# Keys and values held for four query heads, and a position bias kept only where it varies, in a two-layer hybrid attention trunk

## The chip, the cores and the metric

The kernel runs on one core of a Trainium2 chip. The metric is the device time of one execution in microseconds (us); lower is better. The kernel is written against a scheduler that gets instructions in program order, decides in which order each engine runs them, and adds every wait.

## What is computed

The reference is a trunk of two layers over a sequence of 2048 tokens of width 1024, all in float32. Layer 0 mixes tokens in two ways side by side, and only these two matter here. `A` is sliding-window attention with 8 query heads and 2 key/value heads, so four query heads share one pair of keys and values. `B` has 8 heads with keys and values of their own; each 64-token chunk attends to itself and to 8 chunks before it, and a learned bias is added that depends only on the clipped distance.

```python
A_Q_HEADS, A_KV_HEADS, A_WINDOW = 8, 2, 128
B_HEADS, B_PREV_CHUNKS, B_MAX_REL = 8, 8, 128
...
# A: the keys and values of head h // 4, plus a learned sink per head
scores = einsum('bcqhgd,bclhd->bchgql', qc, kb) / sqrt(64)
probs  = softmax(concat([scores, sink]))[..., :-1]
...
# B: bias by distance, clipped to -128 .. 128
rel    = clip(qpos[:, None] - kpos[None, :], -128, 128) + 128
scores = einsum('bcqhd,bclhd->bhcql', qc, kb) / sqrt(64) + rel_table[:, rel]
probs  = softmax(where(valid, scores, -1e30))
```

Layer 1 is differential attention over the whole prefix; the change does not touch it.

## The kernel before

**Stages.** `project(0)` writes queries, keys, values and gates of layer 0 to DRAM scratch tensors. `_mix0` (line 505) then does the attention of layer 0 and its output projection. `project(1)` and `_mix1` do layer 1. Every float32 operand of a matmul is split into a high part H and a low part L, and products are summed over the parts.

**Blocks, heads, rounds.** `_mix0` goes through four blocks of 512 tokens (`b` 0 to 3; `NTB` is 4 tiles of 128). In each it visits 16 heads in rounds of four: two of A, two of B (`heads()`, line 768). Below, A6 and A7 are the A heads of a block's last round and B6, B7 its B heads; B5 is the head just before A6.

**One head.** `load_q` (line 524) loads the queries twice over: `mqd` holds the high parts in both halves of the partitions, `mql` the low parts in both, with two DMAs each. `load_k` (line 536) loads the high parts of the keys into one half of `mks` and the low parts into the other; which half is the high one goes with the parity of the head. `score` (line 544) makes one piece of scores with two matmuls, first with `mqd` (line 547), then with `mql` (line 548). `scores_a` (line 577) loads `mks` and the values `mvA` for every A head. `scores_b` (line 655) loads `mks`, `mvB` and a 128x640 bias, lets POOL write the two masked corners into the bias (lines 667 and 668), and for each 128-token row adds the bias and takes the row's maximum in one DVE instruction per piece (line 682, into `mSP`). ACT then takes the exponential into `mPB` (line 691), POOL scales it (line 693). `values_a` and `values_b` transpose the probabilities on PE (`mtrA` line 640, `mtrB` line 708), split the transposed tile into `mptH` on ACT and `mptL` on DVE (lines 553, 554), and multiply with the values (`mOA`, `mOB`).

**Buffers.** All loads are issued by SP's one queue, in order. A tile with the same tag waits for the release of the tile that many allocations earlier: `qd` has 3 buffers, `ql` 2, `ks` 2, `v` 2 (A and B share `ks` and `v`), `bias` 2, `SP` 2, `PB` 7, `ptH` and `ptL` 4 each. So the `mql` of a head waits for the scores of the head two before it.

**Order.** `pace` (line 48) interleaves three streams: the scores of the heads, the values trailing them by `LAG0` = 9 units, and side work: the last gate products of `project(0)` (`mlg`) and the output projection (`mom`) of finished blocks. The scheduler may still reorder.

Of the kernel before, what the change touches and what calls it, by code (L numbers as in the profile page):

```python
# [10 lines left out]
F32 = mybir.dt.float32  # L11
F32R = mybir.dt.float32r
AF = mybir.ActivationFunctionType
ALU = mybir.AluOpType
# [4 lines left out]
P = 128  # L19
# [4 lines left out]
BLK = NTB * P  # L24
NB = S // BLK
HD = 64
EPS = 1e-6
NEG = -1e30
# [3 lines left out]
def f32(ap):  # L32
    return ap.bitcast(F32)
# [52 lines left out]
class Trunk:  # L86
# [418 lines left out]
    def _mix0(self, es):  # L505
        nc, tc, a, s = self.nc, self.tc, self.a, self.s0
# [26 lines left out]
            nc.sync.dma_start(f32(ql[HD:P, :]), s[L][h // 2, r, tok])  # L533
            res["q"] = (qd, ql)

        def load_k(H, L, p, row, e, k0, k1):

            r = slice(row * HD, (row + 1) * HD)
            ks = ld.tile([P, 1024], F32R, tag="ks", name=n + "ks")
            nc.sync.dma_start(f32(ks[e * HD:(e + 1) * HD, :k1 - k0]), s[H][p, r, k0:k1])  # L540
            nc.sync.dma_start(f32(ks[(1 - e) * HD:(2 - e) * HD, :k1 - k0]), s[L][p, r, k0:k1])
            return ks

        def score(ps, q, j, ks, c0, c1):
            qd, ql = q
# [2 lines left out]
            self.anchor = nc.tensor.matmul(ps, ql[:, js], ks[:, c0:c1], start=False, stop=True).ins  # L548

        def split_pt(ps, wd, tag):  # L550
            H = sb.tile([P, 512], F32R, tag="ptH", name=n + "ptH", bufs=4)
            L = sb.tile([P, 512], F32R, tag="ptL", name=n + "ptL", bufs=4)
            nc.scalar.activation(H[:, :wd], ps[:, :wd], AF.Copy)
            nc.vector.tensor_tensor(L[:, :wd], ps[:, :wd], f32(H[:, :wd]), ALU.subtract)
            return H, L
# [19 lines left out]
            return yH, yL  # L575

        def scores_a(h, b, res):
            g, e = h // 4, h % 2
            k0, k1 = max(0, b * BLK - P), (b + 1) * BLK
# [3 lines left out]
            nc.sync.dma_start(  # L583
                f32(vt[:, :(k1 - k0) // P, :]),
                s["av"][k0:k1, g * 192:(g + 1) * 192].rearrange("(t p) c -> p t c", p=P),
            )
            nm, l, es_, r = small("anm", 4), small("al", 4), small("aes", 4), small("ar", 4)
            pt = sb.tile([P, NTB, 256], F32, tag="PA", name=n + "PA")
            for z in range(2):
# [63 lines left out]
                ys[h // 2] = finish(yt, (h // 2) * P, b)  # L653

        def scores_b(h, b, res):
            e = h % 2
            k0, k1 = max(0, (b - 1) * BLK), (b + 1) * BLK
            load_q("bqH", "bqL", h, b, res)
            ks = load_k("bkH", "bkL", h // 2, e, e, k0, k1)
# [7 lines left out]
            nc.gpsimd.memset(bias[0:HD, 576:640], NEG)  # L667
            nc.gpsimd.memset(bias[HD:P, 0:64], NEG)
            probs = res["p"] = []
            res.update(v=vt, k0=k0)  # L670
            for j in range(NTB):
                t = b * NTB + j
                w0 = max(0, 4 - t) * P
                wd = 640 - w0
                kc = (t - 4) * P + w0 - k0
                sp = sb.tile([P, 640], F32, tag="SP", name=n + "SP")
                cuts = [(0, 320), (320, 640)] if w0 == 0 else [(w0, 640)]
                m, nm, l, r = small("bm", 2), small("bnm"), small("bl"), small("br")
                for z, (ca, cz) in enumerate(cuts):
                    ps = pS.tile([P, 512], F32, tag="S", name=n + "SB")[:, :cz - ca]  # L680
                    score(ps, res["q"], j, ks, kc + ca - w0, kc + cz - w0)
                    nc.vector.tensor_tensor_reduce(
                        sp[:, ca:cz], ps, bias[:, ca:cz], 1.0, NEG, ALU.add, ALU.max, m[:, z:z + 1]
                    )
# [6 lines left out]
                nc.scalar.activation(pb[:, w0:640], sp[:, w0:640], AF.Exp, bias=nm, accum_out=l)  # L691
# [446 lines left out]
def _layout(inputs):  # L1138
# [11 lines left out]
    a["relb"] = np.ascontiguousarray(a.pop("ev_b_rel_bias")[:, rel])  # L1150
    return {k: np.ascontiguousarray(v) for k, v in a.items()}


# [14 lines left out]
```

## Time and profile before

| what | value |
|---|---|
| median of 3 runs | 2955.78 us (2952.22 to 2972.79) |
| the profiled execution, its own time | 2951.96 us |
| its span | 2950.2 us |
| mean granted TensorE clock | 0.972 |
| busy: PE, DVE, ACT, POOL | 2718.6, 1917.2, 1593.5, 1604.6 us |
| DMA traffic | 580.79 MB, mean 197 GB/s |
| heads of `_mix0`, first score to last score | 604.5 to 1152.9 us |
| first scores of the blocks | 604.5, 713.5, 859.4, 1005.5 us |

Times within the trace count from the start of the span. A row of the windows view has, for one stretch, each engine's busy time and number of instructions, the granted TensorE clock as a share of full speed, the share of time in which the DMA engines were busy, and what they moved. A row of the waits view says which group of instructions waited for which other group, for how long in all, how often, and how long at most. In the timeline, the bracket behind a row is the idle time of its engine before it and what ended it. Tile names carry the stage (`m` is `_mix0`); `mks<-akL` is the load of the low parts of A's keys into `mks`.

### The profile page before, as it was taken

The numbers are of one execution on the slowest core, as the hardware profiler recorded it, in microseconds if no ns is written. First come the engines' busy times: TensorE is split into PE (matmuls) and PEld (weight loads), VectorE is DVE, ScalarE is ACT, GpSimd is POOL, SyncE is SP. The second block draws the span as 40 slices with busy tenths as digits, with TensorE's granted clock in tenths as the row PEclk, the third lists the DMA queues.
The fourth block names the chain that finished last, engine by engine and source line by source line (L and its number), as shares of the span: only waits on it lengthen the run. The fifth ranks groups of instructions, "written<-read, shape, count | busy, mean of one in ns | idle before, by whom it ended". The sixth has DMA issues, their size and how long they took to land.

```text
span 2950.2 us, 45159 instructions
## 1 busy us (share of the span) xinstructions
PE 2718.6 (92%) x13672; PEld 2242.1 (76%) x13672; DVE 1917.2 (65%) x4652; ACT 1593.5 (54%) x4135; POOL 1604.6 (54%) x1966
## 2 busy tenths in 40 slices
PE   6999999988888889899999998889999999899888
PEld 5888888876777788777788886667777777677667
DVE  7752385266677676498818861665766888878752
ACT  4443543367556565243334331666766777778752
POOL 3541251245345343267745650776777878789851
PEclk9999999999999999999999998999999999999999
DMA  4773343669988886475895455576768777668863
GB/s 149 230 250 120 113 147 120 197 192 249 262 214 212 216 217 170 146 270 197 259 302 191 127 162 158 164 217 197 225 193 234 200 225 214 176 169 243 221 215 114
DMA packets 427537, 580.79 MB, mean 197 GB/s; under 512 B 48160, under 2 KB 198688, under 8 KB 427296
## 3 DMA queue, kind: packets, MB, share of 16 engines
q1 hardware_dynamic: 427296, 577.92, 66.7%
q8 instruction: 109, 1.79, 0.3%
q14 instruction: 132, 1.08, 0.1%
HBM read 413.14 MB, written 164.63 MB: 196 GB/s over the span
## 4 chain that ended last, share of the span: by engine, by line
PE 63%; DMA 15%; DVE 11%; ACT 4%; POOL 3%; issue 3%; SPq 2%; DVEq 0%; ACTq 0%; POOLq 0%
PE p1mm L216 4%; PE p1mm L214 4%; PE p1mm L215 4%; PE p0mm L215 3%; PE p0mm L216 3%; PE p0mm L214 3%; PE cS L865 3%; PE ctr L912 3%; PE cS L866 3%; DMA mks<-bkL 2%; PE cO L920 2%; PE cG L214 2%; PE cG L216 2%; PE com L214 2%; DVE cnm L869 2%
## 5 line engine op out<-in xcount | busy, mean ns | idle before, releaser
L872 ACT ACTIVATE cP<-cS,cnm 128x512 f32<-128x512 f32 (+3 forms) x640 | 399.0, 630 | 173.8 <-DVE cnm L869 96.0
L869 DVE TENSOR_REDUCE cnm<-cS 128x1 f32<-128x512 f32 (+3 forms) x640 | 374.3, 600 | 100.6 <-PE cS L866 95.4
L865 PE MATMUL cS<-ck,cqd 128*128 128x512 f32 (+3 forms) x640 | 262.9, 415 | 60.0 <-ACT cP L872 20.5
L304 POOL TENSOR_TENSOR p0wL<-p0ws,p0wH 128x512 fp32r<-128x512 f32 (+1 forms) x128 | 155.3, 1246 | 276.0 <-ACT p0wH L303 266.4
L216 PE MATMUL p1mm<-p1wH,p1hL 128*128 128x512 f32 x768 | 303.3, 395 | 0.0
L215 PE MATMUL p1mm<-p1wL,p1hH 128*128 128x512 f32 x768 | 302.9, 395 | 0.4 <-POOL p1wL L304 0.4
L214 PE MATMUL p1mm<-p1wH,p1hH 128*128 128x512 f32 x768 | 302.3, 395 | 0.8 <-ACT p1wH L303 0.8
L899 POOL TENSOR_TENSOR cP<-cP,cP 128x512 f32<-128x512 f32 (+3 forms) x256 | 285.2, 1135 | 0.3
L304 POOL TENSOR_TENSOR p1wL<-p1ws,p1wH 128x512 fp32r<-128x512 f32 x128 | 168.0, 1333 | 136.8 <-ACT p1wH L303 97.5
L214 PE MATMUL p0mm<-p0wH,p0hH 128*128 128x512 f32 (+1 forms) x640 | 237.6, 374 | 3.5 <-ACT p0vt L454 2.6
L866 PE MATMUL cS<-ck,cql 128*128 128x512 f32 (+3 forms) x640 | 235.3, 372 | 3.3 <-DMA cql<-qL 3.3
L215 PE MATMUL p0mm<-p0wL,p0hH 128*128 128x512 f32 (+1 forms) x640 | 238.2, 373 | 0.0
L216 PE MATMUL p0mm<-p0wH,p0hL 128*128 128x512 f32 (+1 forms) x640 | 237.7, 372 | 0.1
L916 DVE TENSOR_TENSOR cptL<-ctr,cptH 128x512 fp32r<-128x512 f32 (+1 forms) x320 | 190.7, 599 | 62.4 <-ACT cptH L915 61.4
L865 PEld LDWEIGHTS cS<-ck,cqd 128*128 128x128 f32 x640 | 123.2, 193 | 104.4 <-ACT cP L872 51.2
L915 ACT ACTIVATE cptH<-ctr 128x512 fp32r<-128x512 f32 (+1 forms) x320 | 169.6, 539 | 58.2 <-PE ctr L912 57.0
L893 POOL TENSOR_SCALAR cP<-cP,ccs 128x512 f32<-128x512 f32 (+3 forms) x288 | 191.9, 683 | 0.0
L912 PE MATMUL ctr<-ident,cP 128*128 128x128 f32 x1088 | 175.4, 277 | 1.4 <-POOL cP L899 1.2
L898 POOL TENSOR_SCALAR cP<-cP,ccs 128x512 f32<-128x512 f32 (+3 forms) x256 | 174.0, 693 | 0.0
L214 PEld LDWEIGHTS p1mm<-p1wH,p1hH 128*128 128x128 f32 x768 | 145.3, 189 | 29.9 <-ACT p1wH L303 1.2
L215 PEld LDWEIGHTS p1mm<-p1wL,p1hH 128*128 128x128 f32 x768 | 145.2, 189 | 29.9 <-POOL p1wL L304 0.8
L216 PEld LDWEIGHTS p1mm<-p1wH,p1hL 128*128 128x128 f32 x768 | 145.4, 189 | 29.3 <-issue 0.2
(321 smaller groups left out, 7719.0 us busy)
## 6 DMA issues: line engine op xcount, KB each, us to landing
p1ws<-in_od_w_in_dram SPq DMA_DIRECT2D x56, 512.0 KB, 4.7
p0ws<-in_ev_w_in_dram SPq DMA_DIRECT2D x48, 512.0 KB, 4.3
ck<-kH SPq DMA_DIRECT2D x160, 128.0 KB, 4.0
ck<-kL SPq DMA_DIRECT2D x160, 128.0 KB, 4.2
cvH<-vH SPq DMA_DIRECT2D x80, 256.0 KB, 3.9
cvL<-vL SPq DMA_DIRECT2D x80, 256.0 KB, 4.7
cqd<-qH SPq DMA_DIRECT2D x128, 128.0 KB, 4.9
cql<-qL SPq DMA_DIRECT2D x128, 128.0 KB, 4.7
```

The lines of the kernel that those rows point to most:

```text
L214: mm(ps, aH, bH, start=first, stop=False)
L215: mm(ps, aH, bL, start=False, stop=False)
L216: mm(ps, aL, bH, start=False, stop=last)
L304: nc.gpsimd.tensor_tensor(l[:, :width], ws[:, k, :width], f32(h[:, :width]), ALU.subtract)
L865: mm(ps, qd[:, m, js], kt[:, :wd], start=True, stop=False)
L866: self.anchor = mm(ps, ql[:, m, js], kt[:, :wd], start=False, stop=True).ins
L869: nc.vector.tensor_reduce(nm[:, m, z:z + 1], ps, AX.X, ALU.max, negate=True)
L872: nc.scalar.activation(chunks[z][:, :wd], ps, AF.Exp, bias=nm[:, m, z:z + 1], accum_out=acc)
L893: nc.gpsimd.tensor_scalar(p1, p1, c1, 1.0, ALU.mult, ALU.mult)
L899: nc.gpsimd.tensor_tensor(p1, p1, p2, ALU.add)
L912: nc.tensor.transpose(tp[:, (j - j0) * P:(j - j0 + 1) * P], us[j][kt // 4][:, kk:kk + P], self.ident)
L916: nc.vector.tensor_tensor(L[:, :wd], tp[:, :wd], f32(H[:, :wd]), ALU.subtract)
```

## The change

Two things change in `_mix0`, and one in the host's table.

1. **A's keys and values.** `load_group` loads them into tiles of their own, `mksA` and `mvA`, with one buffer each, when the first of the four heads that share them comes; the other three use the same tiles. The high parts now always lie in the lower half. `mks` and `v` are left to B.
2. **B's bias.** For distances over 128 the clipped bias is one number per head. The kernel subtracts that number from the whole row (a softmax does not see it), so the first 384 of 640 columns need no bias but the mask, which is one shared tile `edge`. Only 256 columns are loaded per head; POOL subtracts the head's number (`far`, loaded once and negated once by DVE) from them and masks one corner. The row of scores is cut at column 384 (384 and 256 wide) instead of 320, and in block 0, where a row is shorter, two of the four rows now come in two pieces where they came in one. The DVE writes its sum straight into `PB`, the exponential works in place, and the `SP` tile is gone.
3. **Buffers.** `PB` goes from 7 to 8, `ptH` and `ptL` from 4 to 3 each.

```diff
+        edge = ld.tile([P, 384], F32, tag="edge", name=n + "edge", bufs=1)
+        far = ld.tile([P, 8], F32, tag="far", name=n + "far", bufs=1)
+        nc.gpsimd.memset(edge, 0.0)
+        nc.gpsimd.memset(edge[HD:P, 0:64], NEG)
+        nc.sync.dma_start(far, a["relfar"].to_broadcast([P, 8]))
+        nc.vector.tensor_scalar(far, far, -1.0, None, ALU.mult)
+        group = {}
+
+        def load_group(b, g):
+            k0, k1 = max(0, b * BLK - P), (b + 1) * BLK
+            ks = ld.tile([P, 640], F32R, tag="ksA", name=n + "ksA", bufs=1)
+            load_k(ks, "akH", "akL", 0, g, k0, k1)
+            vt = ld.tile([P, 5, 192], F32R, tag="vA", name=n + "vA", bufs=1)
+            nc.sync.dma_start(
+                f32(vt[:, :(k1 - k0) // P, :]),
+                s["av"][k0:k1, g * 192:(g + 1) * 192].rearrange("(t p) c -> p t c", p=P),
+            )
+            return ks, vt, k0
...
-            H = sb.tile([P, 512], F32R, tag="ptH", name=n + "ptH", bufs=4)
-            L = sb.tile([P, 512], F32R, tag="ptL", name=n + "ptL", bufs=4)
+            H = sb.tile([P, 512], F32R, tag="ptH", name=n + "ptH", bufs=3)
+            L = sb.tile([P, 512], F32R, tag="ptL", name=n + "ptL", bufs=3)
...
             load_q("aqH", "aqL", h, b, res)
-            ks = load_k("akH", "akL", 0, g, e, k0, k1)
-            vt = ld.tile([P, 5, 192], F32R, tag="v", name=n + "vA")
...
+            if h % 4 == 0:
+                group[g] = load_group(b, g)
+            ks, vt, k0 = group[g]
...
-            bias = ld.tile([P, 640], F32, tag="bias", name=n + "bias")
+            bias = ld.tile([P, 256], F32, tag="bias", name=n + "bias")
             nc.sync.dma_start(bias, a["relb"][h])
-            nc.gpsimd.memset(bias[0:HD, 576:640], NEG)
-            nc.gpsimd.memset(bias[HD:P, 0:64], NEG)
+            nc.gpsimd.tensor_scalar(bias, bias, 1.0, far[:, h:h + 1], ALU.mult, ALU.add)
+            nc.gpsimd.memset(bias[0:HD, 192:256], NEG)
...
-                sp = sb.tile([P, 640], F32, tag="SP", name=n + "SP")
-                cuts = [(0, 320), (320, 640)] if w0 == 0 else [(w0, 640)]
+                pb = sb.tile([P, 640], F32, tag="PB", name=n + "PB", bufs=8)
+                cuts = [(w0, 384), (384, 640)] if w0 < 384 else [(w0, 640)]
...
-                    nc.vector.tensor_tensor_reduce(
-                        sp[:, ca:cz], ps, bias[:, ca:cz], 1.0, NEG, ALU.add, ALU.max, m[:, z:z + 1]
-                    )
+                    by = edge[:, ca:cz] if ca < 384 else bias[:, ca - 384:cz - 384]
+                    nc.vector.tensor_tensor_reduce(pb[:, ca:cz], ps, by, 1.0, NEG, ALU.add, ALU.max, m[:, z:z + 1])
...
-                pb = sb.tile([P, 640], F32, tag="PB", name=n + "PB", bufs=7)
-                nc.scalar.activation(pb[:, w0:640], sp[:, w0:640], AF.Exp, bias=nm, accum_out=l)
+                nc.scalar.activation(pb[:, w0:640], pb[:, w0:640], AF.Exp, bias=nm, accum_out=l)
```

**What moves on SP's queue.** The place is the last round of block 2, from the moment the scores of B5 are done: the loads for A7 and B6. Before (`mqd_11935` and `mql_11938` are the queries of B6, `mql_11859` those of A7, `mks_11862` and `mks_11941` the keys of A7 and B6):

```order
L529 DMA mqd_11935<-bqH_62 64x512
L532 DMA mql_11859<-aqL_58 64x512
L533 DMA mql_11859<-aqL_58 64x512
L540 DMA mks_11862<-akH_59 64x640
L487 DMA x1_84<-mxr_11506 128x512
L583 DMA mvA_11304<-av_61 128x5x192
L541 DMA mks_11862<-akL_60 64x640
L530 DMA mqd_11935<-bqH_62 64x512
L532 DMA mql_11938<-bqL_63 64x512
L533 DMA mql_11938<-bqL_63 64x512
L540 DMA mks_11941<-bkH_64 64x1024
L661 DMA mvB_11383<-bv_66 128x8x128
```

Now (`mqd_11827` and `mql_11830` are the queries of B6, `mql_11756` those of A7, `mks_11833` the keys of B6):

```order
L539 DMA mks_11833<-bkH_64 64x1024
L676 DMA mvB_11293<-bv_66 128x8x128
L540 DMA mks_11833<-bkL_65 64x1024
L681 DMA mbias_11838<-in_relb_dram 128x256
L529 DMA mqd_11827<-bqH_62 64x512
L532 DMA mql_11756<-aqL_58 64x512
L533 DMA mql_11756<-aqL_58 64x512
L676 DMA mvB_11492<-bv_66 128x8x128
L487 DMA x1_84<-mxr_11414 128x512
L530 DMA mqd_11827<-bqH_62 64x512
L532 DMA mql_11830<-bqL_63 64x512
L533 DMA mql_11830<-bqL_63 64x512
```

A7 has no loads of keys and values left, and B6's keys stand ahead of A7's queries instead of behind B6's.

**What moves on PE.** The place is where A7 begins in the same round. Before, the last rows up to A7's first score (ahead of these, behind B5's last score, stand 12 rows of `mom`, 8 score matmuls of A6, 5 of `mOB` and 15 `mtrA`):

```order
L647 MATMUL mOA<-mptH,mvA 128x128
L649 MATMUL mOA<-mptL,mvA 128x128
L647 MATMUL mOA<-mptH,mvA 128x256
L649 MATMUL mOA<-mptL,mvA 128x256
L647 MATMUL mOA<-mptH,mvA 128x256
L649 MATMUL mOA<-mptL,mvA 128x256
L647 MATMUL mOA<-mptH,mvA 128x256
L649 MATMUL mOA<-mptL,mvA 128x256
L647 MATMUL mOA<-mptH,mvA 128x128
L649 MATMUL mOA<-mptL,mvA 128x128
L640 MATMUL mtrA<-ident,mPA 128x128
L547 MATMUL mSA<-mks,mqd 128x256
```

Now (ahead of these, behind B5's last score, stand 3 rows of `mom`, 8 score matmuls of A6, 2 of `mOB` and 4 `mtrA`):

```order
L567 MATMUL mSA<-mksA,mqd 128x256
L656 MATMUL mtrA<-ident,mPA 128x128 x4
L214 MATMUL mom<-mw,myH 128x512
L215 MATMUL mom<-mw,myH 128x512
L216 MATMUL mom<-mw,myL 128x512
L214 MATMUL mom<-mw,myH 128x512
L215 MATMUL mom<-mw,myH 128x512
L216 MATMUL mom<-mw,myL 128x512
L214 MATMUL mom<-mw,myH 128x512
L215 MATMUL mom<-mw,myH 128x512
L216 MATMUL mom<-mw,myL 128x512
L568 MATMUL mSA<-mksA,mql 128x256
```

A7's scores stand earlier: the ten `mOA` matmuls that stood between B5 and A7 now come behind A7's first scores, so there is less PE work between the end of B5's scores and the first matmul that needs A7's `mql`.

**What moves on DVE.** The place is the first row of B6. Before, the sum goes to `mSP` and stands between the splits of the transposed tiles:

```order
L554 TENSOR_TENSOR mptL_11651<-mtrB_11645,mptH_11650 128x512
L682 ISA mSP_11950,mbm_11951<-mSB_11955,mbias_11946 128x320
L682 ISA mbm_11951 128x1
L554 TENSOR_TENSOR mptL_11666<-mtrB_11660,mptH_11665 128x512
L682 ISA mSP_11950,mbm_11951<-mSB_11959,mbias_11946 128x320
L682 ISA mbm_11951 128x1
```

Now it goes to `mPB_11842`, the buffer that the first row of B4 held until its last transpose (`mtrB_11634` below is that transpose's output):

```order
L574 TENSOR_TENSOR mptL_11570<-mtrB_11564,mptH_11569 128x512
L582 TENSOR_TENSOR myt_11112<-mOA_11451,mlow_11543 64x512
L574 TENSOR_TENSOR mptL_11597<-mtrB_11592,mptH_11596 128x384
L698 ISA mPB_11842,mbm_11843<-mSB_11847,medge_6097 128x384
L698 ISA mbm_11843 128x1
L698 ISA mPB_11842,mbm_11843<-mSB_11851,mbias_11838 128x256
L698 ISA mbm_11843 128x1
L574 TENSOR_TENSOR mptL_11612<-mtrB_11608,mptH_11611 128x256
L574 TENSOR_TENSOR mptL_11637<-mtrB_11634,mptH_11636 128x128
```

The sum of B6's first row has moved behind three splits of B4's values, and two more splits stand behind it.

More of the change, by code (lines that the diff above doesn't have):

```diff
@@ L534, in load_q, with load_k @@
             res["q"] = (qd, ql)
-        def load_k(H, L, p, row, e, k0, k1):
+        def load_k(ks, H, L, p, row, k0, k1):
             r = slice(row * HD, (row + 1) * HD)
-            ks = ld.tile([P, 1024], F32R, tag="ks", name=n + "ks")
-            nc.sync.dma_start(f32(ks[e * HD:(e + 1) * HD, :k1 - k0]), s[H][p, r, k0:k1])
-            nc.sync.dma_start(f32(ks[(1 - e) * HD:(2 - e) * HD, :k1 - k0]), s[L][p, r, k0:k1])
-            return ks
+            nc.sync.dma_start(f32(ks[0:HD, :k1 - k0]), s[H][p, r, k0:k1])
+            nc.sync.dma_start(f32(ks[HD:P, :k1 - k0]), s[L][p, r, k0:k1])
+            return ks
+        edge = ld.tile([P, 384], F32, tag="edge", name=n + "edge", bufs=1)
[15 more added lines that the diff above has]
+            return ks, vt, k0
         def score(ps, q, j, ks, c0, c1):
@@ L577, in scores_a @@
         def scores_a(h, b, res):
-            g, e = h // 4, h % 2
-            k0, k1 = max(0, b * BLK - P), (b + 1) * BLK
+            g = h // 4
             load_q("aqH", "aqL", h, b, res)
-            ks = load_k("akH", "akL", 0, g, e, k0, k1)
-            vt = ld.tile([P, 5, 192], F32R, tag="v", name=n + "vA")
-            nc.sync.dma_start(
-                f32(vt[:, :(k1 - k0) // P, :]),
-                s["av"][k0:k1, g * 192:(g + 1) * 192].rearrange("(t p) c -> p t c", p=P),
-            )
+            if h % 4 == 0:
+                group[g] = load_group(b, g)
+            ks, vt, k0 = group[g]
             nm, l, es_, r = small("anm", 4), small("al", 4), small("aes", 4), small("ar", 4)
@@ L655, in scores_b @@
         def scores_b(h, b, res):
-            e = h % 2
             k0, k1 = max(0, (b - 1) * BLK), (b + 1) * BLK
             load_q("bqH", "bqL", h, b, res)
-            ks = load_k("bkH", "bkL", h // 2, e, e, k0, k1)
+            ks = load_k(ld.tile([P, 1024], F32R, tag="ks", name=n + "ks"), "bkH", "bkL", h // 2, h % 2, k0, k1)
             vt = ld.tile([P, 8, P], F32R, tag="v", name=n + "vB")
```

4 lines of the change are left out of this document (2 added, 2 removed).

## The prediction

> **What bounds the kernel now.** Only `_mix0` changes, so I first read the stage view for where it lies and how busy each engine is in it (block 0, blocks 1 to 3, the tail of the output projection, then `project(1)` beside them).
>
> ```profile
> core 0: us, PE busy (x) PEld busy (x) DVE busy (x) ACT busy (x) POOL busy (x), PEclk, DMA share, GB/s
> 604.00:713.00 109.00, 93.98 (x537) 80.21 (x535) 72.89 (x268) 74.43 (x214) 48.55 (x88) 0.95 0.88 240
> 713.00:859.00 146.00, 120.87 (x717) 105.59 (x718) 103.53 (x367) 91.05 (x244) 64.32 (x100) 0.93 0.93 238
> 859.00:1005.00 146.00, 127.38 (x780) 114.95 (x779) 105.25 (x379) 90.77 (x245) 59.78 (x91) 0.93 0.87 217
> 1005.00:1153.00 148.00, 130.07 (x813) 117.32 (x812) 108.06 (x380) 91.91 (x248) 63.20 (x97) 0.97 0.83 211
> 1153.00:1240.00 87.00, 79.22 (x395) 66.16 (x394) 34.67 (x77) 23.68 (x53) 16.33 (x14) 0.96 0.42 130
> 1240.00:1830.00 590.00, 575.00 (x2681) 472.46 (x2678) 404.90 (x705) 222.88 (x500) 333.33 (x256) 0.99 0.63 207
> ```
>
> PE is the busiest engine, but in the four blocks (549 us) it is idle for 549 - 472 = 77 us; in `project(1)` it is idle for 15 us in 590. DVE is busy about 71% of that time, ACT 63%, POOL 43%: none is the bound by itself. The DMA engines are busy 83 to 93% of the time. Second, the waits view of PE between 604 and 1153 us says what the idle time waits for.
>
> ```profile
> PE mSB L547 <- DMA mks<-bkL: 18.6, 9, 4.7
> PE mSA L547 <- DMA mks<-akL: 12.6, 6, 2.9
> PE mSA L547 <- DMA mqd<-bqH: 7.7, 1, 7.7
> PE mSA L547 <- DMA mks<-akH: 4.5, 3, 2.5
> ...
> PE mSB L547 <- DMA mqd<-bqH: 3.9, 3, 2.5
> PE mSB L547 <- DMA mw<-wo0H: 3.4, 1, 3.4
> PE mSB L547 <- DMA mvB<-bv: 2.9, 1, 2.9
> ...
> PE mSA L547 <- DMA mqd<-aqH: 2.0, 2, 1.4
> ```
>
> These rows add up to 55.6 us, all in front of the first scores of a head, and 35.7 us of them name the keys. With 16 rounds of four heads that is 3.5 us a round. Third, the timeline shows how one such stall comes about. SP's queue, in the last round of block 2, then PE:
>
> ```profile
> 966.25 0.45 SPq L529 DMA_DIRECT2D mqd<-bqH  x1
> 966.79 0.55 SPq L532 DMA_DIRECT2D mql<-aqL  x1
> 967.38 0.59 SPq L533 DMA_DIRECT2D mql<-aqL  x1
> 968.03 0.59 SPq L540 DMA_DIRECT2D mks<-akH  x1
> ...
> 969.78 0.66 SPq L541 DMA_DIRECT2D mks<-akL  x1
> ...
> 973.24 0.30 PE L640 MATMUL mtrA<-ident,mPA 128*128 128x128 f32 x1
> 976.46 0.58 PE L547 MATMUL mSA<-mks,mqd 128*128 128x256 f32 x1 [2.93 <-DMA mks<-akL]
> ```
>
> At 966.25 B5's scores are done, and with them the buffers for A7's `mql` and `mks` come free. The second half of the keys goes out at 969.78, behind four other DMAs, and PE stands from 973.54 until it lands at 976.46. Fourth, what follows a stall:
>
> ```profile
> 968.00:973.00 5.00, 5.00 (x38) 4.56 (x37) 4.50 (x14) 2.93 (x9) 2.90 (x6) 1.00 0.90 234
> 976.50:982.00 5.50, 5.50 (x20) 4.81 (x21) 3.12 (x12) 0.00 (x0) 1.32 (x3) 0.50 1.06 247
> ```
>
> Before it PE ran at the full clock, after it at half, and the number of matmuls in about the same time falls from 38 to 20. So a stall is paid twice: once as idle time, once as half clock behind it.
>
> **Term 1: stalls on loads.** The loads that go, and those that stay (KB each, and us from issue to landing):
>
> ```profile
> mvB<-bv SPq DMA_DIRECT2D x22, 512.0 KB, 7.5
> mvA<-av SPq DMA_DIRECT2D x23, 480.0 KB, 6.0
> mbias<-in_relb_dram SPq DMA_DIRECT2D x30, 320.0 KB, 5.9
> mql<-bqL SPq DMA_DIRECT2D x64, 128.0 KB, 6.1
> ...
> mql<-aqL SPq DMA_DIRECT2D x60, 128.0 KB, 3.8
> ...
> mks<-akH SPq DMA_DIRECT2D x24, 160.0 KB, 4.1
> mks<-akL SPq DMA_DIRECT2D x24, 160.0 KB, 4.6
> ```
>
> Of the 24 A heads of blocks 1 to 3, 18 lose 320 + 480 KB, the 6 in block 0 somewhat less, and 32 biases shrink from 320 to 128 KB: some 25 MB of the 124 that the stages of 549 us move (their widths times their GB/s), a fifth, and 72 issues of about 0.59 us on SP. What PE still waits for is the `mql`, which keeps its two buffers and still goes out only when the head two before is through its scores.
>
> A7's queries: `mql` goes out second and third behind the same event, so its second half starts 967.38 - 966.25 = 1.1 us after it and lands 3.8 us (its own row) to 6.1 us (B's row, from busier moments) later: 4.9 to 7.2 us. Against that stands the PE work between, by the new order 12 `mom`, 9 score, 2 `mOB` and 8 `mtrA` matmuls. Their pitch:
>
> ```profile
> 1050.33 0.39 PE L215 MATMUL mom<-mw,myH 128*128 128x512 f32 x1
> 1050.56 0.39 PE L216 MATMUL mom<-mw,myL 128*128 128x512 f32 x1
> ...
> 1054.44 0.28 PE L547 MATMUL mSA<-mks,mqd 128*128 128x256 f32 x1
> 1054.55 0.28 PE L548 MATMUL mSA<-mks,mql 128*128 128x256 f32 x1
> ```
>
> 12 at 0.23 and 19 at 0.12 us make 5.0 us. The remaining stall is 0 to 2.2 us; nearest is A's own row, so I take 0.5. B6's queries wait for the end of A6's scores, about 2.0 us later; behind A7's `mql` come one `mvB`, a store and half of `mqd`, so the second `mql` starts about 3.7 us after the event and lands at 7.5 to 9.8; PE arrives after 2.0 + 6.5 us (15 `mom`, 26 short matmuls) = 8.5: 0 to 1.3 us, I take 0.5. B6's keys now wait only for B4's scores, nearly a round earlier, and stand ahead in the queue. A round keeps 1.0 of 3.5 us, 16 rounds keep 16: **55.6 - 16 = 40 us gained**; the ends are 56 (all) and 0 (at the 7.5 us of `mvB`'s row A7 alone would wait 3.6 us).
>
> **Term 2: half clock.** The time lost is (1 - PEclk) times the length of each stage: 5 + 10 + 10 + 4 = 30 us; at the 0.99 of `project(1)`, with hardly any stalls, it would be 5. So 0 to 25 us can come back, of which some already lies inside stalls: I take half, **12 us gained**. [...]
>
> **Term 3: what is added.**
>
> ```profile
> L612 POOL TENSOR_SCALAR mPA<-mPA,mar 128x256 f32<-128x256 f32 x128 | 59.0, 479 | 110.1 <-DVE mar L610 74.8 <-ACT mptH L553 14.1 <-PE mom L216 7.3
> ...
> L682 DVE CUSTOM_DVE_ANT_0 mSP<-mSB,mbias 128x128 f32<-128x128 f32 x8 | 2.3, 291 | 6.8 <-DMA mw<-wo0H 3.3 <-POOL mbias L667 1.5 <-POOL mPA L612 1.1
> ...
> ACT mPB L691 <- PE mtrB L708: 18.1, 9, 10.5
> ...
> ACT mptH L553 <- PE mOB L712: 12.2, 5, 4.7
> ```
>
> Block 0 gets 16 more pieces of scores: two matmuls at 0.12 us each, 16 x 0.24 = **4 us lost** on PE. With each comes one more sum on DVE, at least 0.29 us, 5 us in a stage where DVE is idle for 36. Elsewhere 384 + 256 columns are as many as 320 + 320. POOL's subtraction has the shape of the first row: 32 x 0.48 = 15 us, covered by POOL's idle 57%; what it can hold up is the scaling of `mPB` behind it, and without that cover the 15 us would be paid. The wait for a free `PB` buffer moves from ACT (18.1 us) to DVE: 0 to 18 us, I take 1, because the splits that PE waits for next stand ahead of the sum in the new DVE order. With three `ptH` instead of four, ACT may wait more for `mOB` (12.2 us now): 0 to another 12 us, I take 1, since the three transpose banks already hold PE to three tiles. `edge` and `far` are made once, before 604 us, when PE works on gates: nothing.
>
> **Sum.** -40 - 12 + 4 + 1 + 1 = -46 us. The profiled execution took 2951.96 us (span 2950.2), 3.8 less than the median of the three runs; 2951.96 - 46 = **2906 us**, and I give that for the median too.
>
> **The rivals.**
> [...]
> *The queries take the keys' place*: PE now comes to A7 after 5.0 us instead of 7.3, so it only waits earlier. If `mql` lands after 6.1 to 7.5 us (the rows of B's queries and of `mvB`), A7 waits 2.2 to 3.6 us, and B6, reached later for it, not at all: 2.9 x 16 = 46 remain; 10 are gained there, 3 of half clock, 6 lost to term 3: **2945 us**, no change that can be told. For it: the release event is the same as before. Against it: a fifth less traffic should speed the landing.
> *DVE stands for the buffer* (slower): a row's sum now needs its `PB` buffer before it, not after it, and DVE waits in order until PE is through the last transpose of the head two back. Between B6's first score and that transpose lie 8 + 3 + 2 transposes, 3 `mom`, 10 `mOA` and 4 score matmuls, about 4 us. Where the splits stand behind the sum, PE pays; at 1.4 us for each of the 32 B heads the gain is gone, at 3 us for the 24 of blocks 1 to 3 it is 2906 + 72 = **2978 us**. Against it: in the new DVE order three splits stand ahead of the sum, which keep DVE busy until about that transpose.
>
> **How the numbers follow.** Forecast 0.52, the full gain 0.20, no change 0.20, slower 0.08. About 1% (30 us) is what a measurement of this kernel tells from no change; the first two are faster by over 1%: 0.72, 0.20, 0.08. The range goes from a little under the full gain to a little over the third case, 2870 to 2948, which leaves out the slower case and the edges of the others.
>
> **What would show it.** Right: the blocks take some 11 us less each; PE's waits for `mksA` and `mks` together fall under 6 us and some 10 to 16 us name `mql`; PEclk in blocks 1 to 3 rises to 0.95 or more; the DMA share falls below 0.8; layer 1 keeps its length within a few us. Wrong: PE idle stays near 77 us and `mql` heads its waits (queries in the keys' place), DVE's waits on `mtrB` exceed 40 us (the buffer), or PEclk stays at 0.93 with the stalls gone.

## The result, and the profile after

| | before | after |
|---|---|---|
| median of 7 runs each, side by side | 2963.08 us (2952.22 to 2972.79) | 2934.80 us (2926.67 to 2940.84) |
| the profiled execution and its span | 2951.96 us, 2950.2 us | 2935.29 us, 2933.5 us |
| first score to first product of `project(1)` | 604.5 to 1243.0: 638.5 us | 605.6 to 1207.5: 601.9 us |
| last product of `project(1)` to the end | 1826.7 to 2950.2: 1123.5 us | 1790.3 to 2933.5: 1143.2 us |

The changed kernel takes 0.9896 of the time (95% interval 0.9872 to 0.9920), 28 us less. The forecast was 2906, the range 2870 to 2948. The third row, "the stage" from here on, is 37 us shorter. The last row, `_mix1`, is 20 us longer, though the change touches nothing there.

The stage view of the changed kernel, with the cuts at its own blocks (block 0, blocks 1 to 3, the tail, `project(1)`):

```profile
core 0: us, PE busy (x) PEld busy (x) DVE busy (x) ACT busy (x) POOL busy (x), PEclk, DMA share, GB/s
605.00:701.00 96.00, 86.76 (x531) 75.82 (x530) 68.53 (x291) 72.07 (x209) 48.85 (x87) 0.98 0.74 211
701.00:840.00 139.00, 124.73 (x757) 108.70 (x756) 105.51 (x378) 94.76 (x250) 65.09 (x96) 0.96 0.83 216
840.00:978.00 138.00, 127.51 (x795) 111.34 (x793) 112.89 (x384) 93.08 (x248) 64.96 (x97) 0.98 0.75 184
978.00:1118.00 140.00, 128.93 (x807) 113.84 (x806) 114.90 (x379) 93.11 (x245) 65.66 (x98) 0.98 0.68 172
1118.00:1205.00 87.00, 81.45 (x394) 67.86 (x393) 34.21 (x72) 23.85 (x53) 15.51 (x13) 0.94 0.38 118
1205.00:1795.00 590.00, 571.49 (x2676) 469.42 (x2674) 404.23 (x705) 221.48 (x499) 333.09 (x256) 1.00 0.64 207
```

The four blocks take 13, 7, 8 and 8 us less than before. PE is idle in them for 513 - 468 = 45 us, where it was 77, and its clock is 0.96 to 0.98. What they move has fallen from 124 to 100 MB (widths times GB/s). What PE still waits for, from the waits view between 604 and 1140 us:

```profile
PE mSA L568 <- DMA mql<-aqL: 12.5, 6, 3.6
PE mtrB L721 <- DVE mptL L574: 7.0, 17, 1.6
PE mOB L725 <- DVE myt L582: 6.1, 15, 1.0
PE mSB L568 <- DMA mql<-bqL: 4.2, 4, 2.2
PE mSB L567 <- DMA mks<-bkL: 3.3, 1, 3.3
```

A's keys are gone from the list. The queries' low parts stand at its head with 12.5 + 4.2 = 16.7 us, B's keys keep 3.3, and new at this size is DVE: 7.0 + 6.1 = 13.1 us in which a split of a transposed tile or a join of outputs was not done in time. The place that the prediction worked out is A7 in block 2, SP first, then PE:

```profile
942.59 0.45 SPq L529 DMA_DIRECT2D mqd<-bqH  x1
...
943.12 0.55 SPq L532 DMA_DIRECT2D mql<-aqL  x1
...
943.72 0.59 SPq L533 DMA_DIRECT2D mql<-aqL  x1
...
944.70 0.37 PE L567 MATMUL mSA<-mksA,mqd 128*128 128x256 f32 x1
...
948.50 0.39 PE L568 MATMUL mSA<-mksA,mql 128*128 128x256 f32 x1 [0.93 <-DMA mql<-aqL]
```

The second half of A7's `mql` goes out 1.1 us behind the first DMA that B5's end releases and lands 4.8 us later; PE stands for 0.93 us in front of its second score matmul, where before it stood for 2.93 in front of the first. (In a second profile of the changed kernel, below, it stands there for 0.33.)

### The profile page after: what moved, and what is told of

It reads as the page before. It is cut to its first block, busy times and chain, and to the rows that moved or that the text cites. A ratio compares the mean times of both kernels' runs of the same rounds, so it can differ in the third digit from the quotient of the medians.

```text
span 2933.5 us, 45206 instructions
## 1 busy us (share of the span) xinstructions
PE 2726.8 (93%) x13704; PEld 2243.6 (76%) x13704; DVE 1937.4 (66%) x4685; ACT 1595.9 (54%) x4135; POOL 1610.5 (55%) x1968
## 4 chain that ended last, share of the span: by engine, by line
PE 64%; DMA 11%; DVE 11%; ACT 4%; issue 2%; POOL 2%; SPq 1%; DVEq 0%; ACTq 0%; POOLq 0%
PE p1mm L216 4%; PE p1mm L214 4%; PE p1mm L215 4%; PE cS L878 3%; PE cS L879 3%; PE ctr L925 3%; PE p0mm L214 2%; PE p0mm L215 2%; PE p0mm L216 2%; PE cG L214 2%; PE cG L215 2%; PE cG L216 2%; PE cO L933 2%; PE mom L214 2%; PE com L214 2%
## 5 line engine op out<-in xcount | busy, mean ns | idle before, releaser
L878 PE MATMUL cS<-ck,cqd 128*128 128x512 f32 (+3 forms) x640 | 265.7, 420 | 56.4 <-ACT cP L885 19.7
L898 POOL TENSOR_SCALAR ccs<-ce,crl 128x4 f32<-128x4 f32 (+2 forms) x96 | 26.9, 280 | 270.1 <-ACT cP L885 130.1
```

The costliest lines, as they stand in the source:

```text
L878: mm(ps, qd[:, m, js], kt[:, :wd], start=True, stop=False)
```

## The experiments

Each kernel is the kernel before or the changed one with the edit shown. "Stage" is the first score to the first product of `project(1)` in its profiled execution, `_mix1` the last product of `project(1)` to the end.

**The kernel before again.**

> The kernel before, unchanged, for a second profile. The two profiles so far differ by 36 us in the four blocks of _mix0 and by about 20 us the other way in _mix1, which the change does not touch. Theory: the profiled run of before was the lowest of seven and had a short _mix1 by chance; a second one shows the heads of _mix0 at 545 to 552 us again and _mix1 some 5 to 20 us longer than the 1123 of the first. Rival: _mix1 is really faster in the kernel before (its instructions stand in a slightly different order there), and it comes out at 1120 to 1126 again.

2960.51 us, stage 639.8, `_mix1` 1129.7. So the stage is steady (638.5 and 639.8), and 6 of the 20 us of `_mix1` are spread between executions. The first profile of before was a low one: its 2951.96 lies 8 us under the 2960.29 that 29 runs of before gave as a median here. The two profiles also show what a waits view can bear. Between 604 and 1150 us the waits of PE for another engine or a DMA make 72 and 69 us, but those that name a DMA make 58 in the one and 38 in the other, where ACT is named for 20 instead of 7.

**Only the bias.** The changed kernel, with A's keys and values per head as before:

```diff
-            ks = ld.tile([P, 640], F32R, tag="ksA", name=n + "ksA", bufs=1)
+            ks = ld.tile([P, 1024], F32R, tag="ks", name=n + "ks")
-            vt = ld.tile([P, 5, 192], F32R, tag="vA", name=n + "vA", bufs=1)
+            vt = ld.tile([P, 5, 192], F32R, tag="v", name=n + "vA")
-            if h % 4 == 0:
-                group[g] = load_group(b, g)
+            group[g] = load_group(b, g)
```

> Only the second part: the bias of 256 columns, the sum into PB, the three buffers of ptH and ptL; A's keys and values are loaded per head as before. Theory (A's keys and their two shared buffers are what makes the stalls): the waits on mks before A's and B's scores stay, 30 us or more in all, and the kernel is 0 to 8 us faster than before. Rival one (the traffic matters, and 6 of the 25 MB go here): 6 to 12 us faster. Rival two (the gain comes from DVE, ACT and POOL, which this part changes): 20 us or more faster, like the whole change.

2966.04 us, 1.0042 of before (1.0020 to 1.0064): none of the three; it is slower. The stage takes 638.9 us, as before to the microsecond, so the second part alone gains nothing there, though `PB` stands at eight; the 6 us of the total lie behind the stage (`_mix1` 1138.5). The keys' waits stay, in the waits view of this kernel:

```profile
PE mSA L567 <- DMA mks<-akH: 14.5, 5, 4.9
PE mSA L567 <- DMA mks<-akL: 13.3, 6, 4.0
...
PE mSB L567 <- DMA mks<-bkL: 3.6, 3, 1.9
```

The eight `PB` are not simply one more than before: a row now holds its buffer from DVE's sum on, and the two `SP` tiles that held the sum are gone. DVE waits for such a buffer here for 16.6 us:

```profile
DVE mPB L697 <- PE mtrB L720: 16.6, 15, 2.6
```

**Only the keys and values, and its control.** `mksA` and `mvA` take 2.5 and 3.75 KB a partition. In the change the second part and the fewer `ptH` and `ptL` free more than that (two `SP` tiles of 2.5 KB, 3 KB of bias, one `ptH` and one `ptL` of 2 KB each, less 2.5 KB for one more `PB` and 1.5 for `edge`); here both kernels give up buffers for it. The control is the kernel before with:

```diff
-            H = sb.tile([P, 512], F32R, tag="ptH", name=n + "ptH", bufs=4)
-            L = sb.tile([P, 512], F32R, tag="ptL", name=n + "ptL", bufs=4)
+            H = sb.tile([P, 512], F32R, tag="ptH", name=n + "ptH", bufs=3)
+            L = sb.tile([P, 512], F32R, tag="ptL", name=n + "ptL", bufs=3)
-                pb = sb.tile([P, 640], F32, tag="PB", name=n + "PB", bufs=7)
+                pb = sb.tile([P, 640], F32, tag="PB", name=n + "PB", bufs=6)
```

and the other has, beside that, `load_group` as in the change and in `scores_a`:

```diff
-            ks = load_k("akH", "akL", 0, g, e, k0, k1)
-            vt = ld.tile([P, 5, 192], F32R, tag="v", name=n + "vA")
+            if h % 4 == 0:
+                group[g] = load_group(b, g)
+            ks, vt, k0 = group[g]
```

> The kernel before with three buffers each of ptH and ptL and six of PB, a control for the next run, which needs that room. Both theories: within 0 to 8 us slower than before; more would mean that these buffers bind, and then the change has paid for its own three ptH and ptL.

> Only the first part, keys and values held for four heads, on the buffers of the control; bias of 640 columns and SP as before. Theory: nearly the whole gain, 20 to 32 us under the control, stalls that name mks under 8 us, and what remains names mql. Rival (the bias part makes the gain): less than 10 us under the control.

The control: 2974.26 us, 1.0050 of before (1.0029 to 1.0071), stage 657.6, so 18 to 19 us lost by fewer buffers alone, where at most 8 were expected. The keys-and-values kernel: 2949.56 us, 0.9975 of before (0.9954 to 0.9997), 25 us under its control, stage 623.0, which is 35 under. That is the whole change's gain in the stage. Its waits:

```profile
PE mSA L562 <- DMA mql<-aqL: 14.6, 8, 8.6
PE mSB L562 <- DMA mql<-bqL: 11.1, 7, 4.2
PE mOB L721 <- DVE myt L576: 11.0, 10, 5.1
PE mtrB L717 <- POOL mPB L702: 8.1, 12, 1.8
```

No row of it names the keys; 25.7 us name `mql`, and 20.8 us name DVE, where the control has 13.3. The theory holds: the first part makes the gain, and the rest of the change makes the room in which it costs no `PB`. The run does not part the keys from the values, nor the loads that are gone from the two buffers that B now has to itself.

**Which buffer it is.** The kernel before, with the last two lines of the control alone:

> The kernel before with six PB buffers instead of seven: it has nothing of the change, but the scheduler gives layer 1 exactly the order that it has in the changed kernel. Theory (order): _mix1 is 1138 to 1146 us. Rival (layer 1 pays for something of the change itself): 1123 to 1130, as in the kernel before. For the buffers: the control with six PB and three ptH and ptL lost 19 us in layer 0; if PB is what binds, this one loses most of them too, if ptH binds, under 6.

2979.20 us, 1.0079 of before (1.0052 to 1.0107), stage 660.4: all of the control's loss, so `PB` binds and `ptH` does not. PE's waits on the keys in it:

```profile
PE mSB L547 <- DMA mks<-bkL: 20.9, 7, 5.5
PE mSA L547 <- DMA mks<-akL: 19.7, 8, 5.7
PE mSA L547 <- DMA mks<-akH: 9.7, 5, 2.6
```

They name the keys, not the buffer, and more than before (50 against 36 us). The row that does name it does not rise; ACT waits for a free `PB` for 15.8 us with six, and for 18.1 and 16.8 in the two profiles with seven:

```profile
ACT mPB L691 <- PE mtrB L708: 15.8, 10, 5.9
```

One buffer fewer also lets the scheduler place everything anew: by the traces, about half of the 3224 matmuls and transposes that `_mix0` runs ahead of `project(1)` no longer stand in the order that they had. So the loss is that of the buffer and of the order made for it, which no run here parts. The same goes for the buffer experiments below. The keys-and-values kernel is less open to it: about a sixth of these rows stand otherwise there than in its control.

The order theory, which is about layer 1 (last experiment), does not hold here: `_mix1`, in exactly the order of the changed kernel, takes 1131.1 us, where the theory had 1138 to 1146.

**A third buffer for the queries.** The changed kernel with:

```diff
-            ql = ld.tile([P, BLK], F32R, tag="ql", name=n + "ql")
+            ql = ld.tile([P, BLK], F32R, tag="ql", name=n + "ql", bufs=3)
```

> The changed kernel with a third buffer for the low parts of the queries. Theory (what is left of the stalls is queries that go out only when the head two before is through its scores): the waits on mql, 20 us in the changed kernel, fall under 5; layer 0 falls from 602 to 585-592 us. Layer 1 gets the order of the bias-only kernel, some 1138 us. Rival (DVE takes the place: its splits and sums already hold PE for 16 us): PE waits for mtrB and mOB named by DVE rise by as much, and layer 0 stays within 4 us of 602.

2929.13 us, 0.9895 of before (0.9875 to 0.9914), which cannot be told from the changed kernel; stage 602.3.

```profile
PE mtrB L721 <- DVE mptL L574: 6.9, 16, 1.9
PE mOB L725 <- DVE myt L582: 6.6, 17, 0.9
PE mSA L567 <- DMA mqd<-aqH: 6.1, 2, 3.5
PE mom L216 <- POOL myL L594: 4.6, 1, 4.6
PE mSA L567 <- ACT mPA L622: 4.4, 6, 1.0
PE mSB L567 <- ACT mPA L622: 4.1, 3, 2.5
...
PE mSA L568 <- DMA mql<-aqL: 1.7, 2, 1.2
```

The waits on `mql` do fall, from 16.7 to 2.0 us (the row shown and one of 0.3), and nothing is won. The rival has the outcome, but not its reason: DVE's rows stay where they were (18.2 us in all, from 19.7). In place of `mql` stand the high parts of the queries (6.1), POOL, ACT, and 7 to 10 us more at half clock in the stage (47.8, against 37.5 and 41.0 in the two profiles of the changed kernel). Some 40% of PE's rows in `_mix0` stand elsewhere than in the changed kernel.

**And one `PB` buffer fewer.** The same, and in `PB`:

```diff
-                pb = sb.tile([P, 640], F32, tag="PB", name=n + "PB", bufs=8)
+                pb = sb.tile([P, 640], F32, tag="PB", name=n + "PB", bufs=7)
```

> As the run before, and PB at 7 buffers instead of 8. Layer 1 gets exactly the order of the kernel before on every engine. Theory (order): _mix1 comes back to 1123-1130 us; with layer 0 at 590-600 the kernel takes 2900 to 2915 us, and beats the changed kernel by 20 to 35. Rival (layer 1 pays for something else in the change): _mix1 stays at 1138 or more. If one PB buffer fewer costs in layer 0, DVE's waits for mtrB rise from 8 us.

2940.34 us, 0.9934 of before (0.9916 to 0.9953): 5 to 8 us over the medians of the changed kernel, where 20 to 35 under it were expected. The stage takes 619.9 us, 18 more than with eight, while `_mix1` is short, 1129.5.

```profile
PE mtrB L721 <- POOL mPB L706: 23.9, 6, 5.8
PE mtrB L721 <- DVE mptL L574: 11.9, 19, 3.1
```

The wait for the buffer does not show as one: DVE waits for it for 5.2 us, less than the 7.4 with eight, and what PE shows is that it comes to the transposes of a row before POOL has scaled it. That this is because its scores were placed later for want of a buffer is argued, not shown.

**One `PB` buffer more.** The changed kernel with nine, and `sm = pool("sm", 5)` instead of 6 for the room:

> The changed kernel with nine PB buffers instead of eight (and five instead of six buffers of the small tiles, which alone moves no instruction). With seven, beside a third ql, layer 0 was 18 us longer. Theory (eight is where the buffer stops to bind): layer 0 within 4 us of 602. Rival (it still binds): 6 to 15 us shorter. Layer 1 gets an order in which 17 of 7251 PE rows differ from before; by the order theory _mix1 is 1126 to 1134 us, so the kernel gains some 10 us on the changed one either way.

2925.22 us, 0.9887 of before (0.9864 to 0.9909), beside 0.9920 (0.9900 to 0.9941) for the changed kernel in the same comparison: the fastest of all. The stage takes 586.5 us, 15 to 18 less than in the two profiles of the changed kernel, so `PB` still binds at eight and the rival has it, with the order of `_mix0` made anew for it as above. That execution is the lowest of its six (2912.98), so some of the 15 is luck; the medians differ by 7, and no run has the smaller `sm` alone. Blocks 1 to 3 of it:

```profile
700.00:834.00 134.00, 121.99 (x751) 104.97 (x750) 108.74 (x378) 94.52 (x249) 66.79 (x99) 0.99 0.89 227
834.00:969.00 135.00, 125.33 (x796) 110.70 (x795) 110.63 (x385) 93.96 (x249) 65.00 (x96) 0.99 0.77 188
969.00:1105.00 136.00, 130.63 (x835) 115.28 (x834) 114.38 (x388) 95.36 (x253) 67.23 (x99) 1.00 0.70 180
```

DVE is busy for 81 to 84% of these blocks without becoming the bound.

**Traffic or waits: copies in DRAM.** For each A head that loads nothing any more, in the changed kernel:

```diff
+            else:
+                copy_group(b, g, b * 8 + h)    # akH, akL, av -> scratch in DRAM, 800 KB
```

> The changed kernel, and for each of the 24 heads of A that no longer load keys and values the same three transfers again, from the same places in DRAM into a scratch tensor in DRAM that nobody reads: the traffic and SP's issues of before are back, the buffers and waits of the change stay. Theory (the gain is that PE no longer waits for A's keys and the two shared buffers): layer 0 stays within 8 us of 602, and the DMA share of the blocks goes back to 0.8-0.9. Rival (the gain is the traffic, a fifth less): layer 0 goes back up by 20 us or more, with stalls on mql over 40 us. Layer 1 gets the order of the keys-and-values kernel in either case, about 1134 us.

2951.43 us, 0.9968 of before (0.9949 to 0.9986), stage 608.4. This tells nothing of the question: nothing ties the copies to their head, and all 72 went out between 109 and 479 us, beside `project(0)`, which they hold up (first score at 622.3 instead of 605.6 us).

**Traffic or waits: stores.** Tied to the head by what they store:

```diff
+            i = b * 8 + h
+            if h % 4:
+                for z in range(3):
+                    nc.sync.dma_start(s["st"][i, z], pt[:, z:z + 2, :])
```

> The changed kernel, and each of the 24 heads of A that load no keys and values any more stores three pieces of its probabilities, 256 KB each, to a scratch tensor in DRAM that nobody reads: 768 KB a head stand for the 800 KB that the change took away, tied to the head this time, as writes instead of reads. PE's order in layer 0 stays nearly the same (183 of 5269 rows differ). Theory (the gain is that PE does not wait for A's keys and the shared buffers): layer 0 within 8 us of 602. Rival (it is the traffic): 20 us or more above it, with waits on mql and mks over 40 us. Layer 1 gets exactly the order of the kernel before; by the order theory _mix1 is 1123 to 1130 us.

2936.92 us, 0.9933 of before (0.9913 to 0.9952), stage 617.2: 13 to 15 us over the two profiles of the changed kernel, between the two theories. Block 0 and blocks 1 to 3 of it:

```profile
606.00:711.00 105.00, 93.79 (x546) 81.04 (x545) 69.95 (x296) 75.00 (x215) 49.70 (x88) 0.93 0.81 240
711.00:853.00 142.00, 123.69 (x738) 106.27 (x739) 103.14 (x372) 91.85 (x243) 64.11 (x96) 0.96 0.90 244
853.00:993.00 140.00, 130.23 (x799) 113.38 (x798) 114.00 (x385) 93.41 (x250) 64.63 (x97) 0.95 0.80 216
993.00:1134.00 141.00, 129.75 (x797) 113.85 (x796) 114.43 (x376) 92.17 (x243) 66.07 (x98) 0.96 0.74 204
```

8 to 9 of it are in block 0, where the stores carry more than the loads that went (768 against 640 KB a head), 1 to 3 in each other block, and the waits on `mql` are 20.7 us, not over 40. The stores also hold SP's queue, which waits 30.0 us for POOL's scaling:

```profile
SPq L634 <- POOL mPA L629: 30.0, 20, 5.8
```

So the traffic is worth at most some 15 of the 36 us, and the waits and buffers at least 21, provided that a write burdens the DMA engines no less than a read of its size; no run here tests that.

**Layer 1: the order alone, and the changed kernel again.** The order of layer 1's instructions differs between the kernels, because the scheduler comes to it with another state: before against after, 817 of 7251 PE rows of layer 1 in the scheduler's listing. An edit that was to change it and to leave the order of layer 0 alone:

```diff
-        nc.gpsimd.memset(edge, 0.0)
-        nc.gpsimd.memset(edge[HD:P, 0:64], NEG)
+        nc.vector.memset(edge, 0.0)
+        nc.vector.memset(edge[HD:P, 0:64], NEG)
```

> The changed kernel with the two memsets of the edge tile on DVE instead of POOL, ahead of the first block. In layer 0 every other instruction keeps its place on every engine; in layer 1 the scheduler gives the order that the keys-and-values kernel had (20 of 7251 PE rows differ from before) instead of that of the changed kernel (817 differ). Theory (layer 1 pays for the order that the scheduler gives it, not for anything the change does there): _mix1 falls from 1143 to about 1134 us, layer 0 stays at 602 us from first score to the first product of project(1), and the kernel is some 9 us faster than the changed one, ratio to before about 0.986. Rival (the 1143 is chance, or comes from where the new table lies in DRAM): _mix1 stays at 1140 to 1146 and the ratio at 0.9896.

> The changed kernel, unchanged, for a second profile and beside the next ones on the same chip. Theory (layer 1 pays for its order): _mix1 is again the longest of all kernels, 1138 to 1146 us, and layer 0 is 602 within 3. Rival (the 1143 was chance): _mix1 below 1134, like the kernels with other orders.

With the `edge` on DVE: 2931.73 us, 0.9907 of before (0.9884 to 0.9930), stage 600.5, `_mix1` 1131.9. The changed kernel again: 2932.09 us, stage 604.2, `_mix1` 1139.7. The 9 us that the theory expected of the edit do not come in the total. And the edit did not do what was expected of it: in its trace all 7616 PE rows from the first of `project(1)` on stand in the order of the changed kernel, name for name and shape for shape, and so do the rows of layer 1 on DVE, ACT and POOL. So 1131.9 is no effect of another order. It is one more execution of the order that gave 1143.2 and 1139.7.

All kernels side by side, sorted by `_mix1`. The last column is the time in it for which the trace's clock records grant half the clock. The listing's counts of the second column and the traces put the kernels into the same groups, but for the one marked:

| kernel | order of layer 1, PE rows other than before's | `_mix1` | at half clock |
|---|---|---|---|
| before | - | 1123.5 us | 80 us |
| control: `PB` 6, `ptH`, `ptL` 3 | 0 | 1127.6 | 89 |
| changed, `ql` 3 and `PB` 7 | 0 | 1129.5 | 79 |
| before again | - | 1129.7 | 91 |
| before, `PB` 6 | 817 | 1131.1 | 92 |
| changed, `edge` on DVE | 20 expected, as the changed kernel in the trace | 1131.9 | 87 |
| changed, stores | 0 | 1132.3 | 97 |
| changed, copies | 20 | 1133.3 | 93 |
| changed, `PB` 9 | 17 | 1133.7 | 94 |
| keys and values only | 20 | 1133.9 | 85 |
| changed, `ql` 3 | 140 | 1136.3 | 111 |
| bias only | 140 | 1138.5 | 113 |
| changed again | 817 | 1139.7 | 118 |
| changed | 817 | 1143.2 | 115 |

The windows view of `_mix1`, from the kernel before, from the changed one, and from the changed one with the `edge` on DVE:

```profile
1826.70:2950.00 1123.30, 1020.96 (x4930) 805.70 (x4928) 771.57 (x1793) 739.87 (x2049) 808.10 (x1120) 0.96 0.71 201
```

```profile
1790.30:2933.50 1143.20, 1033.95 (x4930) 816.66 (x4928) 781.18 (x1793) 739.41 (x2049) 805.14 (x1120) 0.95 0.70 198
```

```profile
1789.30:2921.20 1131.90, 1026.43 (x4930) 810.71 (x4928) 786.90 (x1793) 739.64 (x2049) 807.44 (x1120) 0.96 0.69 200
```

In the changed kernel the same 4930 matmuls take PE 13 us longer than before, and it is idle for 7 us more. So the lost time is half clock and the gaps around it. Why there is more of it stays open. Four executions in the changed kernel's order take 1131.1 to 1143.2 us, with 87 to 118 us at half clock; five in the order of before take 1123.5 to 1132.3, with 79 to 97. The order may have a share in that, but with the order kept `_mix1` still moves by 9 to 12 us.

## Why the prediction was right, and where it was off

**The bound and the mechanism held.** PE waited for loads, above all for the keys in the two shared buffers (35.7 of 55.6 us). Keys and values held for four heads take these waits away, in the change (3.3 us are left) and alone (no row names the keys, and the stage is 35 us under the control's).

**The number.** That the time lies in the range owes something to its width of 78 us, which takes in the 2945 of *the queries in the keys' place* as well. By its number alone the result, 29 us from the forecast and 10 from that rival, would speak for the rival. What decides against it is the stage, 36 us shorter, and 16.7 us of waits on `mql` where it had 46.

**Term 1, stalls on loads.** 16 us were to stay of 55.6, and 20.0 stayed (16.7 on `mql`, 3.3 on B's keys): a gain of 35.6 against 40. A7, worked out as a stall of 0 to 2.2 us with 0.5 as the choice, stood for 0.93 and 0.33 in the two profiles, and in the first its load took 4.8 us, between the two rows used. (In the stall before, the keys' second half went out behind six other DMAs, not four; no term hangs on it.) What failed is the step from waits to time. The 55.6 came from one profile, and a second gave DMA 20 us less and ACT 13 more with the same stage: between the second profiles the waits that name a DMA fell by 18 us, not 38. And a wait that goes lets another come: the `ql` experiment took 15 us of waits away and moved the stage by 0.4.

**Term 2, half clock.** In the stage, half clock fell from 68.3 to 37.5 us, and from 78.5 to 41.0 in the second profiles. PE's busy time shows what that is worth beside the stalls: 553.1 to 550.4 us and 558.8 to 552.3, with 4 us of added scores in it, so about 7 and 10, against an estimate of 12 with 0 and 25 as the ends.

**Term 3, what is added.** Of the 6 us, 4 were the scores. The other two were for waits that the sum's new place and the third `ptH` would bring. The waits of PE that name DVE rose by far more, from 5.4 to 19.7 us, and from 9.7 to 21.1 in the second profiles. But most of that is not what was added. The keys-and-values kernel, which has the old sum, has 20.8 where its control has 13.3; the bias alone, with the new sum, has 12.4, 3 to 7 more than before. So the term itself was short by a few us, and the rest are waits that come up when those on the keys go, for which the sum has no term. Over all its rows between 604 and 1150 us the view of the first profiles has DMA 38 less, DVE 14 more and the others 4 less. PE's idle time over the stage is the steadier number: 85 and 81 us before, 52 and 52 after.

Forecast for the stage were 46 us; it got 36.6 in the first pair of profiles and 35.6 in the second.

**The base.** The sum was made against 2951.96 us and given for the median too. The medians of before were 2963.08 in the first comparison and 2960.29 and 2959.07 in later ones; against these the forecast sat 7 to 11 us too low.

**Layer 1.** "Layer 1 keeps its length within a few us" was wrong by 10 to 20 us in the profiles. In the medians some 8 of the stage's 36 us are missing at the end (28 and 27 are left), if the stage gains as much in the executions without a profile. So the 29 us between 2906 and 2935 are about 10 in the stage, 8 behind it, and the rest in the base. What makes the 8 stays open (last experiment).

**The rivals.** *The full gain* (-56 for the stalls, -25 for the half clock and 4 for the added scores, 2875 us) did not come: a third of the stalls (20.0 of 55.6 us) and over half of the half clock (37.5 of 68.3) stayed, and DVE, at 76 to 82% in blocks 1 to 3, held PE for some of it (19.7 us of waits). That all 25 us hang on the stalls is shown by no run. *The queries in the keys' place* name what PE now waits for, but at 16.7 us, not 46; the forecast had 10 to 16. *DVE stands for the buffer* is not seen at eight buffers:

```profile
DVE mPB L698 <- PE mtrB L721: 8.3, 10, 2.3
```

8.3 us, not over 40. But its place was well chosen: `PB` does bind in this stage. One more or fewer, with the order that the scheduler made for it, was worth 21 us (seven to six, before), 18 (eight to seven, beside `ql` 3) and 15 (eight to nine, the lowest of six runs). No row that names the buffer follows these steps: DVE waits for it for 5.2 us with seven beside `ql` 3, 7.4 with eight there, 8.3 with eight and 7.3 with nine. The prediction mentions the eighth buffer nowhere as a term; it costed only the wait that moved.

**What was to show it.** Right: waits on the keys under 6 us (3.3), PEclk at 0.95 or more (0.96 to 0.98). Nearly: blocks about 11 us shorter each (13, 7, 8, 8), 16.7 us on `mql`, where 10 to 16 were named, and the DMA share under 0.8 in two of blocks 1 to 3 (0.83, 0.75, 0.68). Wrong: layer 1.

## What to carry to other kernels

Room in SBUF is worth what the tightest buffer makes of it: here the bias edit gained nothing by itself, but together with one `ptH` and one `ptL` given up it paid for the keys' tiles and an eighth `PB`, and one `PB` more or fewer went with 15 to 21 us in the stage while no row that names it followed these steps. A sum of stalls from one profile is no price: for the same 36 us the waits that name a DMA fell by 38 in one pair of profiles and by 18 in the other, and the waits next in line moved up. Take it from two profiles, with the idle time of the stage as the firmer number. And with a scheduler, compare the instruction order of the whole kernel, in the trace that was measured: one buffer more or fewer moved about half of a stage, and an edit that was to change the order of a later stage left it as it was.

## What the runs showed of the hardware

In these traces the granted clock drops to half for 3.4 us at a time. Of 416 stretches at half clock from 600 us on that end before the program does, in the fourteen traces, 251 lasted 3.4 us, 130 lasted 6.8, 19 lasted 10.2 and 16 lasted 13.7, 17.1 or 20.5. A gap of PE of 1 to 3 us is followed by half clock in some cases and not in others. The table counts the gaps that begin at full clock and tells how many are followed by half clock, which is to begin before 3.4 us have gone by behind the gap. Several short gaps often stand close together; the second row has only gaps with less than 0.2 us of other idle time from 3.4 us ahead of them to 3.4 us behind.

| gap of PE | 0.5-1 us | 1-1.5 | 1.5-2 | 2-2.5 | 2.5-3 | 3-3.5 | over 3.5 |
|---|---|---|---|---|---|---|---|
| followed by half clock | 91 of 501 | 40 of 199 | 71 of 130 | 77 of 111 | 47 of 57 | 46 of 54 | 124 of 124 |
| the same, gaps that stand alone | 0 of 165 | 10 of 109 | 23 of 62 | 34 of 61 | 30 of 39 | 37 of 45 | 97 of 97 |

One of them in the changed kernel, a gap of 2.43 us, and the stretches ahead of it and behind it:

```profile
883.45 0.42 PE L663 MATMUL mOA<-mptH,mvA 128*128 128x128 f32 x1 [2.43 <-DVE myt L582]
```

```profile
878.00:881.00 3.00, 2.23 (x17) 1.64 (x15) 2.97 (x6) 1.99 (x7) 3.00 (x4) 1.00 1.11 320
883.50:886.90 3.40, 3.40 (x15) 3.06 (x15) 2.42 (x7) 2.33 (x9) 2.66 (x3) 0.51 0.32 64
```

So a stall of this length may have nothing behind it (27 of the 61 gaps of 2 to 2.5 us that stand alone) or a stretch at half clock (34 of them), which at 3.4 us is worth 1.7 us of work and at 6.8 us 3.4. Among the gaps that stand alone the share rises from 10 of 109 at 1 to 1.5 us to 37 of 45 at 3 to 3.5 us and 97 of 97 over 3.5.
